# Sample queries times state with one stationary operand for all heads, and small matmuls issued as runs, in a two-layer hybrid decoder step

## The chip, the cores and the metric

The kernel runs on one core of a Trainium2 chip. The metric is the device time of one execution in microseconds (us). TensorE appears in the profile as PE (its matmuls) and PEld (the loads of its stationary operand, which overlap the matmuls), VectorE as DVE, ScalarE as ACT, GpSimd as POOL, SyncE as SP.

## The reference, cut to what matters

Two layers; each is a gated feed-forward block, a mixer of four parallel head groups, and a second feed-forward block, with a normalization ahead of each. The tokens are a prompt of 512 and a sample of 8 sequences with 8 tokens each, 576 in all; the prompt starts from an empty state, each sample sequence from a state of its own. Two head groups of the mixer (GLA with four heads of 32 keys, HGRN2 with four heads of 64 keys) follow this recurrence, in chunks:

```python
def step(S, inp):
    qc, kc, vc, gc = inp
    b = jnp.cumsum(gc, axis=1)
    o = jnp.einsum('blhk,bhkv->blhv', qc * jnp.exp(b), S)
    ...
    o = o + jnp.einsum('bijh,bjhv->bihv', att, vc)
    w_end = jnp.exp(b[:, -1:] - b)
    S = S * jnp.exp(b[:, -1])[..., None] + jnp.einsum('bjhk,bjhv->bhkv', kc * w_end, vc)
    return S, o
```

The first `einsum`, queries times the old state, is for the sample one small product for each sequence and head. A third group (SSD) has a recurrence of the same kind, a fourth is a pooling.

## The kernel before, in words

Activations lie with channels on the 128 partitions and tokens along the free dimension. Every large product is made of three matmuls, because each operand is split into a high and a low part (`whi`, `wlo`, and two planes of the activations): lines 255 to 257 (`gemm`), and lines 594 to 596 for the projections that put tokens on the partitions (`proj_tokens`). These are called large matmuls below: 128 rows by 128 columns of the array, 256 to 320 columns streamed. Weights are loaded by DMA and split by ACT (line 194) and DVE (line 195).

In each mixer two generators are interleaved. One is a chain of small dependent steps (`gla`, later `ssd`), the other is a fill of large matmuls (`fill_gla`, `fill_ssd`). After each piece of the fill some steps of the chain are recorded inside `tc.high_priority(offset=...)`; a scheduler then writes one fixed instruction list for each engine, by the instructions' priorities and by when it thinks that their inputs are ready. TensorE works through its list in order.

The chain `gla` goes over five chunks in the order 0, 4, 1, 2, 3; chunk 4 holds the 64 sample tokens, the others 128 prompt tokens. For each chunk `levels` builds the causal weights by doubling block widths: `masked_level` (lines 1157, 1159; widths 1 to 16), lines 1032 and 1034 (widths 32 and 64), and after each level DVE updates `Qg`, `Qh`, `k` and `tree` (lines 1041 to 1048). The diagonal's products are lines 1009 and 1011. Then `finish` handles the chunk before: it transposes the keys (`kt`, lines 1079 and 1077), multiplies weights with values (line 1089) and queries with the old state (line 1091), and forms the state's update (`pu`, line 1111; for the sample line 1133).

Queries times old state of the sample stand at the end of `levels` for chunk 4, line 1063. The state of a head group lies as 128 rows of keys by 64 values for each sequence (`Ss[:, si, b]`; `si` 0 is GLA with all four heads stacked, 1 and 2 are HGRN2 with two heads each). `Qg` and `Qh` hold one copy of the queries for each head, zero in the rows of the other heads, so one stationary operand serves all heads of a group. Before, the heads of even and odd number are written to the lower and the upper 64 partitions of the output, and so each `Ss[:, si, b]` is loaded twice, once for each half: 2 x 3 x 8 = 48 matmuls in a layer, which stream 16 or 8 columns. Their stationary operand is 64 columns wide; others in these steps are 32, 64 or 128 columns wide. ACT copies the result to `ye` (line 1064); DVE scales the sample's state in place only after all 48 have read it (line 1135).

A matmul of float32 operands outside the large ones runs as two passes, two records in the trace; a transpose and the bfloat16 mask product are one.

Of the kernel before, what the change touches and what calls it, by code (L numbers as in the profile page):

```python
# [14 lines left out]
P = 128  # L15
D = 1024
KD = D // P
SEQ = 512
# [18 lines left out]
SSD_AHEAD = 60  # L37
EARLY = 5
# [68 lines left out]
class Trunk:  # L107
# [586 lines left out]

    def fill_gla(self, l, h, gp, vg, vh, xbc, gates):
        nc, I, O = self.nc, self.I, self.O
        v = self.vec[:, l]
        yield
        for dst in (vg, vh):
            self.proj_tokens(h, dst)  # L700
            yield
        yield
        past = gp.tile([P, 6, NB, 3], F32, name="sconv")
        nc.sync.dma_start(past, I["sconv"][l])
        new = gp.tile([P, 6, NB + 1, 3], F32, name="nconv")
        for i in range(6):
            ext = gp.tile([P, EXTC], F32, name="ext", bufs=2)
            nc.gpsimd.memset(ext[:, 0:3], 0.0)
            es = self.ext_sample(ext, 3)
            nc.gpsimd.tensor_copy(es[:, :, 0:3], past[:, i])  # L710
            for hf, t0, n, ps in self.proj(h):
                self.evict_ext(ext, 3, ps, hf, n)
            nc.gpsimd.tensor_copy(new[:, i, 0], ext[:, SEQ:SEQ + 3])
            nc.gpsimd.tensor_copy(new[:, i, 1:], es[:, :, LS:LS + 3])
            acc = gp.tile([P, EXTC - 3], F32, name="acc")
            m = EXTC - 3
            cw = v[:, V_CW + 4 * i:V_CW + 4 * i + 4]
            nc.scalar.activation(acc, ext[:, 0:m], AF.Copy, scale=cw[:, 0:1])
            for q in range(1, 4):
                nc.vector.scalar_tensor_tensor(acc, ext[:, q:q + m], cw[:, q:q + 1], acc, ALU.mult, ALU.add)  # L720
            c = xbc[i]
            b = v[:, V_CB + i:V_CB + i + 1]
            nc.scalar.activation(c[:, :SEQ], acc[:, :SEQ], AF.Silu, bias=b)
            nc.scalar.activation(c[:, SEQ:].rearrange("p (b q) -> p b q", q=LS),
                                 self.ext_rows(acc), AF.Silu, bias=b)
            yield
        nc.sync.dma_start(O["nconv"][l], new)
        for g in gates:
            for hf, t0, n, ps in self.proj(h):
                nc.scalar.activation(g[:, t0:t0 + n], ps[:, :n], AF.Silu)  # L730
            yield
# [84 lines left out]
    def ssd_sample(self, Ss, ye, Cf):  # L816

        nc = self.nc
        ys = self.bank()
        for g in range(2):  # L820
            for b in range(NB):
                k = slice(g * 64 + b * LS, g * 64 + b * LS + LS)
                nc.tensor.matmul(ys[:, k], Ss[:, b, P * g:P * g + P],
                                 Cf[g][:, SEQ + b * LS:SEQ + b * LS + LS], start=True, stop=True)
        nc.scalar.copy(ye, ys[:, :P])

    def ssd(self, l, sp, pre, xbc, Ss, ye):
# [13 lines left out]
        for c in (0, 4, 1, 2, 3):  # L841
# [4 lines left out]
            for t in range(2):  # L846
                nc.tensor.transpose(xt[:n, P * t:P * t + P], xs[t][:, q], self.ident)
                nc.tensor.transpose(xt[:n, 256 + P * t:256 + P * t + P], Bf[t][:, q], self.ident)
            wt = self.bank()
            nc.tensor.transpose(wt[:n, 0:8], W8[:, q], self.ident[64:72, 64:72])  # L850
# [15 lines left out]
            nc.tensor.matmul(pe4, L8[:, q], rx[:, :, :n], start=True, stop=False)  # L866
            nc.tensor.matmul(pe4, self.identb[:n, :n],
                             (self.smask if smp else self.cmask)[:n, :n].unsqueeze(1).to_broadcast([n, 4, n]),
                             start=False, stop=True)
# [3 lines left out]
            for g in range(2):  # L873
                nc.tensor.matmul(cb[:n, g * n:g * n + n], Bf[g][:, q], Cf[g][:, q], start=True, stop=True)
# [5 lines left out]
            for hh in range(4):  # L880
                r0 = 64 * (hh % 2)
                nc.tensor.matmul(yi[r0:r0 + 64, (hh // 2) * n:(hh // 2) * n + n], xd[:n, hh], att[:n, hh, :n],
                                 start=True, stop=True)
            yc = sp.tile([P, 2, P], F32, name="yc")
            yi2 = yi[:, 0:2 * n].rearrange("p (t i) -> p t i", i=n)
            if c > 0:
                pd = self.bank("lv")
                for t in range(2):
                    nc.tensor.matmul(pd[:, t * n:t * n + n], sel[:, P * t:P * t + P], cum[:, q],
                                     start=True, stop=True)  # L890
                ecb = sp.tile([P, 2, P], F32, name="ecb")
                nc.scalar.activation(ecb[:, :, :n], pd[:, 0:2 * n].rearrange("p (t i) -> p t i", i=n), AF.Exp)
                if not smp:
                    ye = self.bank()
                    for g in range(2):
                        nc.tensor.matmul(ye[:, g * n:g * n + n], S[:, P * g:P * g + P], Cf[g][:, q],
                                         start=True, stop=True)
# [7 lines left out]
            if not smp:  # L905
                pu = self.bank()
                for g in range(2):
                    nc.tensor.matmul(pu[:, P * g:P * g + P], bt[:, P * g:P * g + P],
                                     xw[:, 2 * g:2 * g + 2], start=True, stop=True)
# [71 lines left out]
    def gla(self, l, gp, f3, q3, k3, vg, vh, o3):  # L981
# [8 lines left out]
        def levels(c, st):  # L990
# [18 lines left out]
            nc.tensor.matmul(sd[r, 0:4], qk[:, 0, :n], hg, start=True, stop=True)  # L1009
            for t in range(2):  # L1010
                nc.tensor.matmul(sd[r, 4 + 2 * t:6 + 2 * t], qk[:, 1 + t, :n], h2, start=True, stop=True)
# [11 lines left out]
            while w < blk:  # L1023
# [6 lines left out]
                for j0 in range(0, n if w >= 32 else 0, 2 * w):  # L1030
                    j, i = slice(j0, j0 + w), slice(j0 + w, j0 + 2 * w)
                    nc.tensor.matmul(lv[j, 0:4 * w], kc[:, 0, j], Qg[:, :, i], start=True, stop=True)
                    for t in range(2):
                        nc.tensor.matmul(lv[j, (4 + 2 * t) * w:(6 + 2 * t) * w], kc[:, 1 + t, j], Qh[:, t, :, i],
                                         start=True, stop=True)
                    nc.scalar.copy(att[j, :, i], lv[j, 0:8 * w].rearrange("p (s w) -> p s w", w=w))
# [17 lines left out]
            if smp:  # L1054
                ys = self.bank()
                y4 = ys[:, :4 * n].rearrange("p (t i) -> p t i", i=n)
                for r0 in (0, 64):
                    odd = r0 // 64
                    for t0, t1, si, Q in ((0, 2, 0, Qg[:, odd::2]), (2, 3, 1, Qh[:, 0, odd:odd + 1]),
                                          (3, 4, 2, Qh[:, 1, odd:odd + 1])):  # L1060
                        for b in range(NB):
                            k = slice(b * LS, b * LS + LS)
                            nc.tensor.matmul(y4[r0:r0 + 64, t0:t1, k], Ss[:, si, b], Q[:, :, k], start=True, stop=True)  # L1063
                nc.scalar.copy(ye, ys[:, :4 * n])
                yield

        def finish(c, st):
# [15 lines left out]
            for s in range(8):  # L1083
                t, r0 = s // 2, 64 * (s % 2)
                val = vg[c][r, 64 * s:64 * s + 64] if s < 4 else vh[c][r, 64 * (s - 4):64 * (s - 4) + 64]
                Q = Qg[:, s] if s < 4 else Qh[:, t - 2, s % 2]
                si = 0 if s < 4 else t - 1
                out = po[r0:r0 + 64, t * n:t * n + n]
# [14 lines left out]
            if not smp:  # L1103
                pu = self.bank()
                for s in range(8):
                    if s < 4:
                        rr, si, d, val = slice(32 * s, 32 * s + 32), 0, 32, vg[c][:, 64 * s:64 * s + 64]
                    else:
                        si = 1 + (s - 4) // 2
                        rr, d, val = slice(64 * (s % 2), 64 * (s % 2) + 64), 64, vh[c][:, 64 * (s - 4):64 * (s - 4) + 64]  # L1110
                    nc.tensor.matmul(pu[rr, 64 * si:64 * si + 64], kw[:, si, rr], val, start=True, stop=True)
# [41 lines left out]
    def masked_level(self, lv, r, c0, lev, n, w, kc, g2, h2v, a2):  # L1153
# [3 lines left out]
        nc.tensor.matmul(lv[r, 0:4 * half], kc[:, 0], g2, start=True, stop=True)  # L1157
        for t in range(2):
            nc.tensor.matmul(lv[r, (4 + 2 * t) * half:(6 + 2 * t) * half], kc[:, 1 + t], h2v[t],
                             start=True, stop=True)  # L1160
# [40 lines left out]
    def group_norm(self, gp, src, groups, width, finish):  # L1201
# [5 lines left out]
        for hf, (_, n) in enumerate(HALVES):  # L1207
# [4 lines left out]
            for t in range(nt):  # L1212
                sq = self.tmp.tile([P, 320], F32, name="sq", tag="sq", bufs=2)
                nc.scalar.activation(sq[:, :n], src(t, hf), AF.Square)
                for c, t0 in enumerate(toks):
                    nc.tensor.matmul(s3[:, c, per * t:per * t + per], sq[:, t0:t0 + P], sel, start=True, stop=True)
# [289 lines left out]
```

## Time and profile before

| what | value |
|---|---|
| time, median of 3 runs | 2357.5 us (2356.81 to 2359.22) |
| time of the profiled execution | 2355.57 us, span 2353.8 us |
| mean granted TensorE clock, share of full | 0.980 |
| PE busy | 2313.3 us, 98% of the span |
| DVE busy / ACT busy | 1618.1 us, 69% / 1004.7 us, 43% |
| DMA | 189.93 MB, mean 81 GB/s |

The span goes from the first to the last instruction; 1.8 us of the profiled execution lie outside it. Busy time is the union of an engine's instructions, so a busy PE need not be streaming: a matmul's record lasts longer than its share of the pipeline, and what counts is the distance from one start to the next.

### The profile page before, as it was taken

The page shows a single profiled execution, that of the slowest core. Times are in us where ns is not written, and L with a number is a line of the kernel's source. Part 1 is how long each engine was busy: PE and PEld are TensorE (multiplying, and loading weights), DVE is VectorE, ACT ScalarE, POOL GpSimd, SP SyncE. Part 2 cuts the span into 40 slices and gives each one's busy share as a digit, 9 for nine tenths or more (in the row PEclk, how much of TensorE's full clock was granted, in tenths as well). Part 3 has the DMA queues.
Part 4 walks back from the last instruction along what each step waited for, and adds up shares of the span by engine and source line. Part 5 has one row for each costly group of instructions (what it writes and reads, how often), then busy time and mean ns, then how long its engine had stood idle before and what let it go on. Part 6 is the DMA issues. An engine that isn't in the chain of part 4 may idle for free.

```text
span 2353.8 us, 40838 instructions
## 1 busy us (share of the span) xinstructions
PE 2313.3 (98%) x16817; PEld 2200.9 (94%) x16817; DVE 1618.1 (69%) x3049; ACT 1004.7 (43%) x1834; POOL 44.9 (2%) x94
## 2 busy tenths in 40 slices
PE   7999999999999999999999999999999999999997
PEld 6999999987888999999999999999778899999997
DVE  8776666746657877667697675767374778767575
ACT  3453444622434544344454343546244435434352
POOL 1000000000010000000000000000000100000000
PEclk9999999998999999999999999999799999999998
DMA  4232323201212133232313323232112131332322
GB/s 152 84 94 83 102 81 108 69 28 50 69 39 92 56 108 92 80 108 72 117 46 99 108 73 99 68 110 63 37 42 75 57 113 37 97 101 75 96 75 74
DMA packets 63147, 189.93 MB, mean 81 GB/s; under 512 B 7120, under 2 KB 13552, under 8 KB 62448
## 3 DMA queue, kind: packets, MB, share of 16 engines
q1 hardware_dynamic: 62816, 187.31, 25.1%
q8 instruction: 132, 2.16, 0.4%
q14 instruction: 55, 0.45, 0.1%
q10 hardware_dynamic: 144, 0.00, 0.0%
HBM read 180.36 MB, written 6.93 MB: 80 GB/s over the span
## 4 chain that ended last, share of the span: by engine, by line
PE 89%; DVE 6%; ACT 3%; DMA 2%; issue 1%; ACTq 0%; DVEq 0%; SPq 0%
PE mm L257 20%; PE mm L255 20%; PE mm L256 20%; PE lv L255 3%; PE lv L257 3%; PE lv L256 3%; DVE wlo L195 2%; PE ms L257 2%; PE ms L256 2%; PE ms L255 2%; DMA raw<-wts 1%; ACT whi L194 1%; PE mm L595 1%; PE mm L596 1%; PE mm L594 1%; PE ms L1063 1%
## 5 line engine op out<-in xcount | busy, mean ns | idle before, releaser
L255 PE MATMUL mm<-h,whi 128*128 128x288 f32 (+2 forms) x1872 | 566.9, 304 | 11.8 <-ACT h L126 6.8
L257 PE MATMUL mm<-h,whi 128*128 128x288 f32 (+2 forms) x1872 | 562.3, 303 | 3.8 <-DVE h L127 3.8
L256 PE MATMUL mm<-h,wlo 128*128 128x288 f32 (+2 forms) x1872 | 563.8, 302 | 0.6 <-DVE wlo L195 0.6
L195 DVE TENSOR_TENSOR wlo<-raw,whi 128x1024 fp32r<-128x1024 f32 (+2 forms) x296 | 315.9, 1069 | 224.2 <-ACT whi L194 222.9
L255 PE MATMUL mm<-a,whi 128*128 128x256 f32 (+2 forms) x1408 | 414.5, 295 | 1.7 <-ACT a L277 1.7
L257 PE MATMUL mm<-a,whi 128*128 128x256 f32 (+2 forms) x1408 | 414.1, 295 | 0.5
L256 PE MATMUL mm<-a,wlo 128*128 128x256 f32 (+2 forms) x1408 | 414.4, 294 | 0.0
L255 PEld LDWEIGHTS mm<-h,whi 128*128 128x128 f32 x1872 | 358.3, 192 | 25.2 <-issue 10.6
L194 ACT CAST whi<-raw 128x1024 fp32r<-128x1024 f32 (+2 forms) x296 | 271.9, 921 | 249.8 <-PE mm L257 195.6
L257 PEld LDWEIGHTS mm<-h,whi 128*128 128x128 f32 x1872 | 356.5, 191 | 14.7 <-issue 7.9
L256 PEld LDWEIGHTS mm<-h,wlo 128*128 128x128 f32 x1872 | 358.0, 192 | 11.9 <-issue 10.6
L194 ACT CAST whi<-raws 128x1024 fp32r<-128x1024 f32 x195 | 204.6, 1049 | 179.3 <-PE mm L257 149.2
L195 DVE TENSOR_TENSOR wlo<-raws,whi 128x1024 fp32r<-128x1024 f32 x195 | 238.1, 1221 | 55.3 <-ACT whi L194 55.0
L257 PEld LDWEIGHTS mm<-a,whi 128*128 128x128 f32 x1408 | 263.7, 188 | 4.3 <-DVE a L278 4.3
L255 PEld LDWEIGHTS mm<-a,whi 128*128 128x128 f32 x1408 | 264.7, 188 | 2.4 <-ACT a L277 2.4
L256 PEld LDWEIGHTS mm<-a,wlo 128*128 128x128 f32 x1408 | 264.7, 188 | 0.0
L429 DVE SCALAR_TENSOR_TENSOR x<-mm,x 128x320 f32<-128x320 f32 (+2 forms) x256 | 116.5, 456 | 157.7 <-PE mm L257 157.0
L255 PE MATMUL mm<-more,whi 128*128 128x288 f32 x624 | 184.8, 296 | 0.5 <-ACT u L487 0.4
L256 PE MATMUL mm<-more,wlo 128*128 128x288 f32 x624 | 184.8, 296 | 0.3 <-DVE wlo L195 0.3
L257 PE MATMUL mm<-more,whi 128*128 128x288 f32 x624 | 184.9, 297 | 0.0
L255 PEld LDWEIGHTS mm<-more,whi 128*128 128x128 f32 x624 | 117.3, 188 | 1.5 <-ACT more L277 0.7
L256 PEld LDWEIGHTS mm<-more,wlo 128*128 128x128 f32 x624 | 117.5, 188 | 0.5 <-DVE wlo L195 0.5
(334 smaller groups left out, 3967.1 us busy)
## 6 DMA issues: line engine op xcount, KB each, us to landing
raw<-wts SPq DMA_DIRECT2D x156, 512.0 KB, 3.7
raw<-wts SPq DMA_DIRECT2D x106, 384.0 KB, 3.1
raws<-wts SPq DMA_DIRECT2D x78, 512.0 KB, 4.4
raw<-wts SPq DMA_DIRECT2D x32, 256.0 KB, 2.7
x<-x SPq DMA_DIRECT2D x4, 576.0 KB, 5.2
Ss<-sssm SPq DMA_DIRECT2D x2, 1024.0 KB, 6.5
nssm_s<-Ss SPq DMA_DIRECT2D x2, 1024.0 KB, 4.1
y<-x SPq DMA_DIRECT2D x4, 320.0 KB, 2.4
```

The source lines that it names most:

```text
L194: nc.scalar.copy(hi[:, :n], src[:, :n])
L195: nc.vector.tensor_tensor(lo[:, :n], src[:, :n], hi[:, :n].bitcast(F32), ALU.subtract)
L255: mm(ps[:, :n], wh, ah, start=(first and i == 0), stop=False)
L256: mm(ps[:, :n], wl, ah, start=False, stop=False)
L257: mm(ps[:, :n], wh, al, start=False, stop=(final and i == last))
L429: self.nc.vector.scalar_tensor_tensor(x, pd[:, :n], 0.5, x, ALU.mult, ALU.add)
L594: nc.tensor.matmul(ps[:, :256], ah, wh, start=(k == 0), stop=False)
L595: nc.tensor.matmul(ps[:, :256], ah, wl, start=False, stop=False)
L596: nc.tensor.matmul(ps[:, :256], al, wh, start=False, stop=(k == KD - 1))
L1063: nc.tensor.matmul(y4[r0:r0 + 64, t0:t1, k], Ss[:, si, b], Q[:, :, k], start=True, stop=True)
```

## The change

It has two parts. The sample's queries meet the state with each `Ss[:, si, b]` loaded once: all heads of a group are streamed together (32 columns for GLA, 16 for each half of HGRN2), and the lower and the upper 64 partitions of the output now hold the sequences 0 to 3 and 4 to 7, in alternation. That makes 24 matmuls in a layer; four ACT copies put the result into the former layout of `ye` where one did. The other part puts the small matmuls of a step into `with self.burst():`, which raises their priority by 300 places, so that the scheduler writes them down next to each other; in `finish` the order within a pair of heads is changed as well, first the two products with values, then the two with the old state.

```diff
+BURST = 300
...
+    def burst(self):
+
+        return self.tc.high_priority(offset=BURST)
...
             if smp:
                 ys = self.bank()
-                y4 = ys[:, :4 * n].rearrange("p (t i) -> p t i", i=n)
-                for r0 in (0, 64):
-                    odd = r0 // 64
-                    for t0, t1, si, Q in ((0, 2, 0, Qg[:, odd::2]), (2, 3, 1, Qh[:, 0, odd:odd + 1]),
-                                          (3, 4, 2, Qh[:, 1, odd:odd + 1])):
-                        for b in range(NB):
-                            k = slice(b * LS, b * LS + LS)
-                            nc.tensor.matmul(y4[r0:r0 + 64, t0:t1, k], Ss[:, si, b], Q[:, :, k], start=True, stop=True)
-                nc.scalar.copy(ye, ys[:, :4 * n])
+                y4 = ys[:, :256].rearrange("p (s b q) -> p s b q", b=4, q=LS)
+                with self.burst():
+                    for s0, s1, si, Q in ((0, 4, 0, Qg), (4, 6, 1, Qh[:, 0]), (6, 8, 2, Qh[:, 1])):
+                        for b in (0, 4, 1, 5, 2, 6, 3, 7):
+                            r0 = 64 * (b // 4)
+                            nc.tensor.matmul(y4[r0:r0 + 64, s0:s1, b % 4], Ss[:, si, b], Q[:, :, b * LS:b * LS + LS],
+                                             start=True, stop=True)
+                y2 = ys[:, :256].rearrange("p (t odd i) -> p odd t i", odd=2, i=32)
+                yo = ye.rearrange("p (t bh i) -> p bh t i", bh=2, i=32)
+                for odd in range(2):
+                    for bh in range(2):
+                        nc.scalar.copy(yo[64 * odd:64 * odd + 64, bh], y2[64 * bh:64 * bh + 64, odd])
                 yield
...
             kt = self.bank()
-            for t in range(3):
-                if smp:
-                    nc.tensor.matmul(kt[r, P * t:P * t + P], kc[:, t], self.ident, start=True, stop=True)
-                else:
-                    nc.tensor.transpose(kt[:, P * t:P * t + P], kc[:, t], self.ident)
+            with self.burst():
+                for t in range(3):
+                    if smp:
+                        nc.tensor.matmul(kt[r, P * t:P * t + P], kc[:, t], self.ident, start=True, stop=True)
+                    else:
+                        nc.tensor.transpose(kt[:, P * t:P * t + P], kc[:, t], self.ident)
...
-            for s in range(8):
-                t, r0 = s // 2, 64 * (s % 2)
...
-                nc.tensor.matmul(out, val, att[r, s, :n], start=True, stop=(c in (0, 4)))
-                if 0 < c < 4:
-                    nc.tensor.matmul(out, S3[:, si], Q, start=False, stop=True)
-                if s == 3:
+            old = 0 < c < 4
+            for t in range(4):
+                si = max(t - 1, 0)
+                for late in range(1 + old):
+                    for s in (2 * t, 2 * t + 1):
...
+                        with self.burst():
+                            if late:
+                                nc.tensor.matmul(out, S3[:, si], Q, start=False, stop=True)
+                            else:
+                                nc.tensor.matmul(out, val, att[r, s, :n], start=True, stop=not old)
+                if t == 1:
                     yield
```

The same `with self.burst():` goes around the matmuls of lines 1009 and 1011, 1032 and 1034, 1111, 1157 and 1159 in the GLA chain, around those of `ssd` and `ssd_sample` (lines 823, 847 to 850, 866 and 867, 874, 882, 889, 896, 908) and of `group_norm` (line 1216), with nothing else altered there. The matmuls that update the sample's state (lines 928 and 1133) are not wrapped.

In the whole program the PE list has 1000 small matmuls before and 952 after. Before they stand in 364 runs between large matmuls, 174 of these of a single matmul; after in 198 runs, 24 of a single one. Where the stationary operand's width (128, 64 or 32 columns) differs from that of the matmul before, the array changes its division into column tiles: 448 times before, 232 times after.

On PE, in the first layer's mixer, where chunk 4 reaches line 1063 (`S3s` is the sample's state, `Qh` HGRN2's queries, rows with `whi` or `wlo` are large matmuls of the values' projection), the list before alternates:

```order
L1011 MATMUL ms<-cst,qk 128x2 x2
L1063 MATMUL ms<-Qh,S3s 64x8
L594 MATMUL mm<-whi,h_4552 128x256
L1063 MATMUL ms<-Qh,S3s 64x8
L595 MATMUL mm<-wlo,h_4552 128x256
L1063 MATMUL ms<-Qh,S3s 64x8
L596 MATMUL mm<-whi,h_4552 128x256
```

The same place after the change (lines are 13 to 25 higher there: 1076 is the sample's product, 1098 the transposes, 1114 weights times values, 1135 the state's update, 1184 a level):

```order
L596 MATMUL mm<-wlo,h_4557 128x256
L1076 MATMUL ms<-Qg,S3s 64x4x8
L1098 MATMUL ms<-cst,k_4683 128x128
...
L1114 MATMUL ms<-att,vg_4684 64x128 x4
...
L1076 MATMUL ms<-Qg,S3s 64x4x8 x2
L1184 MATMUL lv<-Qh,k_4683 128x128
L1135 MATMUL ms<-vg_4684,kw 32x64 x4
L1076 MATMUL ms<-Qg,S3s 64x4x8
L1076 MATMUL ms<-Qh,S3s 64x2x8 x16
L597 MATMUL mm<-whi,h_4557 128x256
```

Rows that only repeat are left out there: eight GLA loads stand among three transposes, four products with values, two level matmuls and four of the state's update, twelve changes of width in all; the sixteen HGRN2 loads follow as one piece, and no large matmul stands between the first and the last of the 24.

On PE, the finishing step of prompt chunk 2 before (`S` is the prompt's state, `att` the weights, `vg` and `vh` the values); the pattern goes on in the same way:

```order
L1079 MATMUL ms<-cst,k_4683 128x128
L256 MATMUL mm<-h_4557,wlo 128x256
L1089 MATMUL ms<-att,vg_4686 64x128
L257 MATMUL mm<-h_4557,whi 128x256
L1091 MATMUL ms<-Qg,S_5156 64x128
L1111 MATMUL ms<-vg_4686,kw 32x64 x4
L1111 MATMUL ms<-vh_4691,kw 64x64 x2
L255 MATMUL mm<-h_4522,whi 128x320
```

And after:

```order
L1098 MATMUL ms<-cst,k_4683 128x128 x2
L1114 MATMUL ms<-att,vg_4686 64x128 x2
L1112 MATMUL ms<-Qg,S_5156 64x128 x2
...
L1112 MATMUL ms<-Qh,S_5156 64x128 x2
L1098 MATMUL ms<-cst,k_4683 128x128
L258 MATMUL mm<-h_4522,whi 128x256
...
L1135 MATMUL ms<-vg_4686,kw 32x64 x4
L1135 MATMUL ms<-vh_4691,kw 64x64 x4
```

Where ten large matmuls and two level steps stood among the pieces of this step, one run holds the transposes and the sixteen products, and after seven large matmuls a second run holds the state's update.

## Rows read from the trace of the kernel before

**Rows 1.** The page: busy time by engine, and the granted clock in 40 slices.
```profile
PE 2313.3 (98%) x16817; PEld 2200.9 (94%) x16817; DVE 1618.1 (69%) x3049; ACT 1004.7 (43%) x1834; POOL 44.9 (2%) x94
...
PEclk9999999998999999999999999999799999999998
```

**Rows 2.** Busy time and granted clock by stretch of the first layer's mixer.
```profile
core 0: us, PE busy (x) PEld busy (x) DVE busy (x) ACT busy (x) POOL busy (x), PEclk, DMA share, GB/s
505.00:514.92 9.92, 9.92 (x83) 7.50 (x82) 2.81 (x9) 1.84 (x6) 0.00 (x0) 1.00 0.01 2
514.92:540.95 26.03, 26.03 (x112) 18.81 (x112) 6.24 (x7) 5.34 (x13) 0.00 (x0) 0.57 0.08 22
540.95:545.75 4.80, 4.80 (x23) 4.62 (x21) 1.49 (x5) 0.00 (x0) 0.00 (x0) 0.50 0.26 102
...
675.47:682.28 6.81, 6.81 (x27) 5.38 (x27) 5.89 (x19) 1.62 (x2) 2.33 (x2) 0.50 0.21 68
692.54:695.93 3.39, 3.39 (x15) 2.96 (x15) 1.49 (x4) 0.69 (x3) 2.06 (x2) 0.50 0.01 3
545.75:630.00 84.25, 83.71 (x586) 64.21 (x586) 62.29 (x148) 32.23 (x76) 4.34 (x18) 1.00 0.13 42
```

**Rows 3.** Line 1063 alone: its matmuls, and who waited for it.
```profile
L1063 PE MATMUL ms<-Qh,S3s x128: 202/256/276, 514.4 to 1697.4; 128*64 128x8 f32 x128
...
  DVE S3s L1135: 31.9, 2
```

**Rows 4.** Timeline of PE, large matmuls ahead of it: start, duration, instruction.
```profile
504.70 0.28 PE L595 MATMUL mm<-wlo,h 128*128 128x256 f32 x1
504.82 0.28 PE L596 MATMUL mm<-whi,h 128*128 128x256 f32 x1
```

**Rows 5.** Timeline of PE in the alternation, at full clock.
```profile
515.44 0.28 PE L1063 MATMUL ms<-Qh,S3s 128*64 128x8 f32 x2
...
515.97 0.28 PE L1063 MATMUL ms<-Qh,S3s 128*64 128x8 f32 x2
```

**Rows 6.** The same farther on; the third row is eight loads in one run.
```profile
519.51 0.38 PE L1063 MATMUL ms<-Qh,S3s 128*64 128x8 f32 x2
...
520.34 0.39 PE L1063 MATMUL ms<-Qh,S3s 128*64 128x8 f32 x2
...
536.98 1.88 PE L1063 MATMUL ms<-Qh,S3s 128*64 128x8 f32 x16
```

**Rows 7.** Timeline of PE, the finishing step of chunk 3, one run.
```profile
626.76 0.49 PE L1079 MATMUL ms<-cst,k 128*128 128x128 f32 x3
627.18 0.45 PE L1089 MATMUL ms<-att,vg 128*64 128x128 f32 x4
...
629.13 0.32 PE L1111 MATMUL ms<-vg,kw 128*32 128x64 f32 x8
629.38 0.45 PE L1111 MATMUL ms<-vh,kw 128*64 128x64 f32 x8
629.76 0.41 PE L255 MATMUL mm<-h,whi 128*128 128x320 f32 x1
```

**Rows 8.** Timeline of PE, the finishing step of chunk 2, in pieces.
```profile
606.57 0.27 PE L1079 MATMUL ms<-cst,k 128*128 128x128 f32 x1
...
612.02 0.42 PE L255 MATMUL mm<-h,whi 128*128 128x320 f32 x1
...
612.73 0.42 PE L256 MATMUL mm<-h,wlo 128*128 128x320 f32 x1
...
616.24 0.42 PE L255 MATMUL mm<-h,whi 128*128 128x320 f32 x1
```

**Rows 9.** Timeline of PE, one level step of full width.
```profile
467.64 0.61 PE L1157 MATMUL lv<-Qg,k 128*128 128x256 f32 x2
...
468.47 0.40 PE L255 MATMUL mm<-h,whi 128*128 128x320 f32 x1
```

**Rows 10.** Who PE waited for: us in total, times, longest.
```profile
PE lv L1157 <- DVE k L1046: 1.9, 5, 0.8
```

More of the change, by code (lines that the diff above doesn't have):

```diff
@@ L872, in ssd @@
             cb = self.bank()
-            for g in range(2):
-                nc.tensor.matmul(cb[:n, g * n:g * n + n], Bf[g][:, q], Cf[g][:, q], start=True, stop=True)
+            with self.burst():
+                for g in range(2):
+                    nc.tensor.matmul(cb[:n, g * n:g * n + n], Bf[g][:, q], Cf[g][:, q], start=True, stop=True)
             for g in range(2):
@@ L879, in ssd @@
             yi = self.bank("lv")
[L880 to L883, printed above, removed]
+            with self.burst():
+                for hh in range(4):
+                    r0 = 64 * (hh % 2)
+                    nc.tensor.matmul(yi[r0:r0 + 64, (hh // 2) * n:(hh // 2) * n + n], xd[:n, hh], att[:n, hh, :n],
+                                     start=True, stop=True)
             yc = sp.tile([P, 2, P], F32, name="yc")
@@ L887, in ssd @@
                 pd = self.bank("lv")
-                for t in range(2):
-                    nc.tensor.matmul(pd[:, t * n:t * n + n], sel[:, P * t:P * t + P], cum[:, q],
-                                     start=True, stop=True)
+                with self.burst():
+                    for t in range(2):
+                        nc.tensor.matmul(pd[:, t * n:t * n + n], sel[:, P * t:P * t + P], cum[:, q],
+                                         start=True, stop=True)
                 ecb = sp.tile([P, 2, P], F32, name="ecb")
@@ L894, in ssd @@
                     ye = self.bank()
[L895 to L897 removed]
+                    with self.burst():
+                        for g in range(2):
+                            nc.tensor.matmul(ye[:, g * n:g * n + n], S[:, P * g:P * g + P], Cf[g][:, q],
+                                             start=True, stop=True)
                 nc.vector.tensor_tensor(yc[:, :, :n], ecb[:, :, :n],
@@ L906, in ssd @@
                 pu = self.bank()
-                for g in range(2):
-                    nc.tensor.matmul(pu[:, P * g:P * g + P], bt[:, P * g:P * g + P],
-                                     xw[:, 2 * g:2 * g + 2], start=True, stop=True)
+                with self.burst():
+                    for g in range(2):
+                        nc.tensor.matmul(pu[:, P * g:P * g + P], bt[:, P * g:P * g + P],
+                                         xw[:, 2 * g:2 * g + 2], start=True, stop=True)
                 S4 = S.rearrange("p (h d) -> p h d", d=64)
@@ L1031, in levels @@
                     j, i = slice(j0, j0 + w), slice(j0 + w, j0 + 2 * w)
[L1032 to L1035, printed above, removed]
+                    with self.burst():
+                        nc.tensor.matmul(lv[j, 0:4 * w], kc[:, 0, j], Qg[:, :, i], start=True, stop=True)
+                        for t in range(2):
+                            nc.tensor.matmul(lv[j, (4 + 2 * t) * w:(6 + 2 * t) * w], kc[:, 1 + t, j], Qh[:, t, :, i],
+                                             start=True, stop=True)
                     nc.scalar.copy(att[j, :, i], lv[j, 0:8 * w].rearrange("p (s w) -> p s w", w=w))
@@ L1104, in finish @@
                 pu = self.bank()
[L1105 to L1111, printed above, removed]
+                with self.burst():
+                    for s in range(8):
+                        if s < 4:
+                            rr, si, d, val = slice(32 * s, 32 * s + 32), 0, 32, vg[c][:, 64 * s:64 * s + 64]
+                        else:
+                            si = 1 + (s - 4) // 2
+                            rr, d, val = slice(64 * (s % 2), 64 * (s % 2) + 64), 64, vh[c][:, 64 * (s - 4):64 * (s - 4) + 64]
+                        nc.tensor.matmul(pu[rr, 64 * si:64 * si + 64], kw[:, si, rr], val, start=True, stop=True)
                 pu3 = pu[:, 0:192].rearrange("p (t d) -> p t d", d=64)
@@ L1156, in masked_level @@
         half, nb = n // 2, n // (2 * w)
[L1157 to L1160, printed above, removed]
+        with self.burst():
+            nc.tensor.matmul(lv[r, 0:4 * half], kc[:, 0], g2, start=True, stop=True)
+            for t in range(2):
+                nc.tensor.matmul(lv[r, (4 + 2 * t) * half:(6 + 2 * t) * half], kc[:, 1 + t], h2v[t],
+                                 start=True, stop=True)
         mask = self.lmask[r, lev, c0:c0 + half].rearrange("p (o b w) -> p o b w", o=1, w=w)
@@ L1214, in group_norm @@
                 nc.scalar.activation(sq[:, :n], src(t, hf), AF.Square)
-                for c, t0 in enumerate(toks):
-                    nc.tensor.matmul(s3[:, c, per * t:per * t + per], sq[:, t0:t0 + P], sel, start=True, stop=True)
+                with self.burst():
+                    for c, t0 in enumerate(toks):
+                        nc.tensor.matmul(s3[:, c, per * t:per * t + per], sq[:, t0:t0 + P], sel, start=True, stop=True)
             r = self.tmp.tile([P, 24], F32, name="gr", tag="gr", bufs=2)
```

46 lines of the change are left out of this document (25 added, 21 removed).

## The prediction

> **What bounds the kernel now.** I read the page first: TensorE is busy for 98% of the span, DVE for 69%, ACT for 43%, so a term of the sum must be time on TensorE [rows 1]. The same page shows the granted clock at nine tenths or more almost everywhere, and at 7 in one slice that lies in the second layer's mixer. I then took the first mixer by stretches. From 514.92 to 540.95 us TensorE is busy without a gap, but only 112 matmuls start or run there and the clock is 0.57; DVE works 6.2 of the 26 us [rows 2]. TensorE is not waiting for anything; it is doing little per microsecond. The view of line 1063 names the work: the sample's queries times state. DVE waits 31.9 us for it, 16 us in each layer [rows 3].
>
> The timeline gives the price. Two large matmuls in a row start 0.12 us apart [rows 4]. In the alternation one large matmul and one 64-column load with its two passes take 515.97 - 515.44 = 0.53 us [rows 5], and 0.83 us after the clock has fallen to half [rows 6]. The load itself is not what costs: eight of them in one run, still at half clock, take 538.79 - 536.98 = 1.81 us (1.88 with the drain), so 0.11 for a pass, about 0.055 at full clock [rows 6]. What remains of the 0.53 is 0.53 - 0.12 - 2 x 0.055 = 0.30, two changes between 128 and 64 columns, 0.15 each.
>
> The finishing steps give the same comparison without the clock. Chunk 3 finds no large matmul ready beside it, and its 51 records stand in one run: 629.76 - 626.76 = 3.00 us [rows 7]. Chunk 2 does the same work in pieces, from 606.57 to 616.24, 9.67 us [rows 8]. In between stand ten large matmuls (four of 256 columns at 0.12, six of 320 at 0.15: 1.4 us) and two level steps at 468.47 - 467.64 = 0.83 [rows 9]. That leaves 9.67 - 1.4 - 1.7 = 6.6 us: the pieces cost 3.6 us.
>
> **The change, part by part.**
>
> *Sample queries.* In the stretch 514.92 to 540.95 stand 39 of the layer's 48 loads (78 of the 112 records) and some 33 large matmuls. At full clock and undisturbed those take 33 x 0.12 = 4.0 us, so the 39 loads cost 26.0 - 4.0 = 22.0. The other nine stand in the 9.92 us ahead of it [rows 2], mixed with a finishing step. Its dense price there, from the sizes above (nine large matmuls 1.1, two level steps 1.7, transposes 0.4, eight products with values at half of 629.13 - 627.18, so 1.0, the state's update 0.6 [rows 7], the diagonal 0.9) is 5.7, so 4.2 are owed to those nine and to the pieces. Behind the stretch the clock stays at half for another 4.8 us [rows 2], of which half, 2.4, is lost. Together 28.6 us a layer.
>
> After, 24 loads remain: 48 passes, without a large matmul in between, in a run with twelve changes of width. Alternating halves is cheaper than one half: the eight passes of the HGRN2 update, alternating, take 629.76 - 629.38 = 0.38 with the change at their end [rows 7], so 0.03 each. I take 48 x 0.03 = 1.4 plus 12 x 0.15 = 1.8, and 0.5 because the values' products of that step are now split over two runs: 3.7. Bounds: no overlap of the halves, 48 x 0.055 = 2.6, which is 1.2 more; and all at half clock, 48 x 0.11 = 5.3. The four ACT copies in place of one lie on an engine that works 5.3 of these 26 us and hold a result that DVE wants only steps later; nothing if that cover is there, under a microsecond a layer if not. Saved: 28.6 - 3.7 = 24.9 a layer, 49.8 in all.
>
> The Trainium skill, TensorE: Matmul & The Clock Gate, section Part 3: Packing small matmuls, says that a load of a stationary operand overlaps matmuls in flight only when the two use different groups of rows. All 24 loads use all 128 rows, so by that rule the halves would not overlap and the saving would be 2 x 1.2 = 2.4 us smaller; the trace has 0.03 against 0.055 for the same operand width and does not agree, and I follow the trace.
>
> *Finishing steps.* Chunk 2 falls from 6.6 to the dense 3.0 plus one more run (0.3) and one change (0.15): 3.1 saved. Chunk 1 stands in the same pieces before; after, the diagonal's products stand between its state updates, six more changes of width, 0.9, so 2.3. Chunk 3 was dense and is now two runs: 0.5 lost. In the sample's finishing step and in the first chunk's narrow levels lone runs are merged, twelve become five; at the 0.3 of two changes, 7 x 0.3 = 2.1. Per layer 7.0, in all 14.0.
>
> *Other wrapped steps.* Most are 128 columns wide like the large matmuls, so that merging them takes no change of width away. In the SSD steps the number of changes of width is the same within two (54 and 56 by the list). I take 0, with 4 us either way.
>
> *What comes back.* Two things are not in the sum. The clock can still fall: behind other stretches of small matmuls it stands at 0.50 for 3.4 and 6.8 us [rows 2], a loss of half of that. I take one such fall more in a mixer, 2.5 us, 5 in all (0 if none). And TensorE now reaches the next level sooner; DVE's update of `k` is what it waits for there today, 1.9 us in all [rows 10]. I take 1 us more.
>
> Sum: 49.8 + 14.0 + 0 - 5 - 1 = 57.8. The profiled execution took 2355.6, 1.8 of it outside the span and untouched; 2355.6 - 57.8 = 2297.8. It lies 1.9 below the median of the runs shown, so for a median I say **2299**.
>
> **The rivals.**
>
> *DVE sets the pace* (0.20). Levels follow one another: TensorE, then DVE's updates, then TensorE. Against it: from 545.75 to 630 DVE is busy 62.3 of 84.25 us, 74%, and with the savings there it would be some 80%; in the 26 us of the alternation it has 20 us to spare [rows 2]. For it: the 25 us a layer that go are just the ones in which DVE could catch up, and its longest wait today is 0.8 us at one level [rows 10]. There are 31 levels in a layer; 0.4 us more on each of 62 is 25 us back: 2299 + 25 = 2324.
>
> *The clock falls as long as before* (0.12). The fall began in the alternation, between 515.97 and 519.51 [rows 5, 6], and lasted to 545.75 [rows 2], some 27 us; at 0.83 for 0.53 it took about 10 of them. If the new run brings the same, 20 less the 5 counted above come back: 2298 + 15 + 1.9 = 2314. The Trainium skill, TensorE: Matmul & The Clock Gate, section Why this matters for your kernels, says that thin matmuls make the clock swing unless they are issued contiguously along the contraction, which speaks for this. In the rows here two short falls stand for it, and against it that the finishing step of chunk 3, dense as it is, lies in a stretch with the clock at 1.00 [rows 2, 7].
>
> *More than the sum* (0.08): no fall of the clock in the mixers at all, and the SSD merges worth their 4 us: 70 us, 2287.
>
> *Slower* (0.04). TensorE works in order, and a run that is written down up to 300 places earlier stands ahead of large matmuls that are ready. If DVE is late for it, those queue behind it, and the evictions that free their PSUM banks with them. To eat 58 us the 198 runs must wait 0.3 us each beyond today; at 0.35 the time is 2355.6 - 58 + 69 = 2367. Today's longest wait of that kind is 0.8 us, at five places in all [rows 10], so I give it little.
>
> *No change* (0.02): only if these waits and the saving cancel, since the new list does have half the changes of width (448 to 232).
>
> **How the numbers follow.** The forecast, 50 to 66 us off, 2291 to 2307, has 0.54. A range from 2284 to 2330 takes in the bounds of the sum, the clock rival and the DVE rival up to 0.5 us on each level; outside stay the slower cases, the worst of the DVE rival and the best of "more", about 0.13. About 0.2%, 5 us, is what a measurement of this kernel can tell from no change. Faster by more than that: 0.54 + 0.20 + 0.12 + 0.08 = 0.94; same 0.02; slower 0.04.
>
> **What the new profile would show.** Line 1076 with 48 records a layer within some 5 us, and DVE's wait for it (16 us at line 1135) gone; the clock at 0.9 or more in the slices of both mixers where 0.7 and 0.8 stand; finishing steps of chunks 1 and 2 as runs of 2 to 3.5 us; feed-forward stretches of the same length as before. Wrong would be: large matmuls that wait for DVE or ACT in the mixers for over 10 us in all, half clock for over 10 us in a mixer beyond the two falls of today, or DVE busy near 95% between the sample's product and the end of the GLA chain.

## The result, and the profile after

The changed kernel takes 2301.9 us (median of 4 runs, 2297.56 to 2308.58), the kernel before 2358.2 on the same chip (4 runs, 2356.81 to 2359.22): a ratio of 0.9764, with a 95% interval of 0.974 to 0.9789, 56 us less. The forecast was 2299 in a range from 2284 to 2330. The profiled execution is one of 2301.8 us, with a span of 2300.0.

From the page of the kernel after, the rows that answer to [rows 1]:

```profile
PE 2253.3 (98%) x16721; PEld 2168.6 (94%) x16721; DVE 1619.4 (70%) x3049; ACT 1010.7 (44%) x1844; POOL 45.6 (2%) x94
...
PEclk9999999999989999999999999999999899999998
```

TensorE is busy for 60 us less and still for 98% of a shorter span; DVE's work is the same. The slices at 7 and 8 where the sample's product stood read 9; of the three that now read 8, the first two lie in the SSD steps.

The sample's product in the kernel after, busy time and granted clock by stretch (columns as in [rows 2]), and line 1076 with its last waiter:

```profile
493.15:498.41 5.26, 5.26 (x75) 4.08 (x74) 3.42 (x13) 0.59 (x2) 0.00 (x0) 1.00 0.01 3
498.41:597.00 98.59, 97.47 (x756) 81.28 (x756) 71.03 (x165) 40.60 (x99) 5.19 (x18) 1.00 0.16 52
...
L1076 PE MATMUL ms<-Qh,S3s x64: 209/209/230, 497.0 to 1630.3; 128*64 128x16 f32 x64
...
  DVE S3s L1159: 0.5, 2
```

All 24 loads of the first layer, part of a finishing step and two level products fit into 5.3 us at a clock of 1.00, and it stays at 1.00 for the 98 us behind; before, 30.8 us went by at 0.57 and 0.50 [rows 2]. The 31.9 us for which DVE waited [rows 3] are 0.5. DVE is busy for 71.0 of those 98.6 us, 72%.

Timeline of PE after: the end of that run, then the finishing step of chunk 2, against [rows 7, 8]:

```profile
497.13 1.14 PE L1076 MATMUL ms<-Qh,S3s 128*64 128x16 f32 x31
498.19 0.38 PE L597 MATMUL mm<-whi,h 128*128 128x256 f32 x1
...
569.79 0.38 PE L1098 MATMUL ms<-cst,k 128*128 128x128 f32 x2
570.10 0.44 PE L1114 MATMUL ms<-att,vg 128*64 128x128 f32 x4
...
572.00 0.33 PE L1098 MATMUL ms<-cst,k 128*128 128x128 f32 x1
572.09 0.36 PE L258 MATMUL mm<-h,whi 128*128 128x256 f32 x1
...
573.10 0.32 PE L1135 MATMUL ms<-vg,kw 128*32 128x64 f32 x8
573.35 0.45 PE L1135 MATMUL ms<-vh,kw 128*64 128x64 f32 x8
573.73 0.39 PE L256 MATMUL mm<-h,whi 128*128 128x256 f32 x1
```

31 passes of the sample's product take 498.19 - 497.13 = 1.06 us, 0.03 each. Chunk 2's step takes 572.09 - 569.79 = 2.30 and 573.73 - 573.10 = 0.63 us, 2.9 where the pieces cost 6.6.

Not all is gain. Who PE waited for after (us in total, times, longest):

```profile
PE ms L1252 <- DVE wide L1249: 4.2, 6, 1.4
...
PE lv L1182 <- DVE k L1061: 3.3, 7, 0.8
PE lv L874 <- DVE yc L912: 2.9, 2, 2.2
```

The level's wait for `k` grew by 1.4 us [rows 10]. The other two lie in the group norm and in the SSD steps.

The stretches at half clock (a granted clock of 0.50) in the two mixers, in all, before and then after:

```profile
518.45:545.76 27.31, 27.31 (x112) 20.83 (x112) 7.05 (x10) 3.33 (x6) 0.00 (x0) 0.50 0.13 39
...
sum 75.10, PE 75.10 PEld 58.42 DVE 28.96 ACT 11.28 POOL 8.80; mean PE 12.52 PEld 9.74 DVE 4.83 ACT 1.88 POOL 1.47
```

```profile
653.45:660.28 6.83, 6.83 (x32) 6.58 (x32) 3.38 (x11) 1.06 (x4) 0.00 (x0) 0.50 0.00 0
673.93:680.76 6.83, 6.83 (x24) 5.88 (x23) 2.27 (x5) 0.60 (x1) 0.00 (x0) 0.50 0.18 58
...
sum 27.31, PE 27.31 PEld 25.86 DVE 13.95 ACT 3.10 POOL 1.92; mean PE 6.83 PEld 6.47 DVE 3.49 ACT 0.77 POOL 0.48
```

Before, 27.31 us a layer (one row of two) belong to the sample's product; that is gone. The remaining stretches lie in the SSD steps: 75.10 - 2 x 27.31 = 20.5 us before, 27.3 after. The mean granted clock of the change's four executions went from 0.988 (2308.6 us) to 0.991 (2297.6 us), so a few us of half clock come and go between executions of one kernel, and a difference of that size between two profiles shows little.

### The profile page after: what moved, and what is told of

Read it like the earlier page. It is cut to its first block, busy times and chain, and to the rows that moved or that the text cites. A ratio compares the mean times of both kernels' runs of the same rounds, so it can differ in the third digit from the quotient of the medians.

```text
span 2300.0 us, 40667 instructions
## 1 busy us (share of the span) xinstructions
PE 2253.3 (98%) x16721; PEld 2168.6 (94%) x16721; DVE 1619.4 (70%) x3049; ACT 1010.7 (44%) x1844; POOL 45.6 (2%) x94
## 4 chain that ended last, share of the span: by engine, by line
PE 88%; DVE 7%; ACT 3%; DMA 1%; issue 1%; POOL 0%; ACTq 0%; DVEq 0%; SPq 0%
PE mm L258 21%; PE mm L256 21%; PE mm L257 20%; PE lv L256 3%; PE lv L258 3%; PE lv L257 3%; PE ms L258 2%; PE ms L257 2%; PE ms L256 2%; DVE wlo L196 1%; ACT whi L195 1%; PE lv L1182 1%; DMA raw<-wts 1%; DVE att L1187 1%; PE ms L1157 1%
## 5 line engine op out<-in xcount | busy, mean ns | idle before, releaser
L256 PEld LDWEIGHTS mm<-h,whi 128*128 128x128 f32 x1872 | 357.6, 191 | 24.1 <-issue 10.6
```

Source lines behind the costliest of these rows:

```text
L256: mm(ps[:, :n], wh, ah, start=(first and i == 0), stop=False)
```

## The experiments

Each ratio is against runs of the kernel before on the same chip; the last column is the ratio less 1, times 2358.

| kernel | median us | ratio, 95% interval | us against before |
|---|---|---|---|
| half_loads | 2336.3 | 0.9905 (0.9892 to 0.9919) | -22 |
| run_of_48 | 2334.0 | 0.9897 (0.9883 to 0.9910) | -24 |
| half_loads_run | 2319.2 | 0.9825 (0.9812 to 0.9838) | -41 |
| wide_48 | 2349.1 | 0.9960 (0.9947 to 0.9972) | -9 |
| one_half_at_a_time | 2317.8 | 0.9828 (0.9814 to 0.9841) | -41 |
| old_sample_in_runs | 2320.1 | 0.9842 (0.9825 to 0.9860) | -37 |
| no_finish_runs | 2320.7 | 0.9847 (0.9833 to 0.9860) | -36 |
| the change | 2301.9 | 0.9764 (0.9740 to 0.9789) | -56 |
| no_norm_runs | 2298.6 | 0.9748 (0.9733 to 0.9764) | -59 |
| no_ssd_runs | 2294.5 | 0.9733 (0.9719 to 0.9747) | -63 |
| runs_in_gla_only | 2292.0 | 0.9719 (0.9705 to 0.9732) | -66 |
| gla_wide_12 | 2292.6 | 0.9727 (0.9712 to 0.9743) | -64 |
| gla_no_level_runs | 2287.9 | 0.9707 (0.9690 to 0.9724) | -69 |

**Loads and run, each alone.** The theory was the prediction's: a lone load among large matmuls costs two changes of width, the alternation also brings the clock down, and both loads and run count. The rivals: only the order matters, or only the number of loads.

half_loads is the kernel before with the new product, not in a run:

```diff
-                for r0 in (0, 64):
...
+                for s0, s1, si, Q in ((0, 4, 0, Qg), (4, 6, 1, Qh[:, 0]), (6, 8, 2, Qh[:, 1])):
+                    for b in (0, 4, 1, 5, 2, 6, 3, 7):
```

> The kernel before with the sample's product alone changed (24 loads in a layer in place of 48, with the four copies), and no run: the loads still alternate with large matmuls. Width theory (each lone load costs two changes of width, 0.30 us, besides its two passes, and the alternation brings the clock down): half the loads save half of 48 x 0.41 = 9.8 us a layer, and about half of the 10 us that the clock fall costs, so 30 us in all, 2328 us. Order theory (only that the loads stand in one run matters): 24 x 0.11 us less a layer, 2353 us. Load theory (only their number matters): as low as the whole change, near 2306 us.

run_of_48 is the kernel before with one line ahead of the old loops, half_loads_run has both edits:

```diff
+                with self.tc.high_priority(offset=300):
```

> The kernel before with its 48 loads of the sample's product in one run of raised priority, nothing else changed. Width theory: 96 passes at 0.055 us (blocks of one half do not alternate) and two changes of width, 5.6 us a layer in place of some 28, so 45 us less, 2313 us. Order theory: the same as with 24 loads in a run, about 2308 us. Load theory: no change, 2358 us. Clock rival (a dense run of thin matmuls lets the clock fall as long as the alternation did): 2313 + 20 = 2333 us, and a fall to half clock of some 20 us behind the run.

> The kernel before with the sample's product as after, 24 loads in one run, and no other run. Width theory: 48 passes at 0.03 to 0.055 us and two changes of width, 2 to 3 us a layer in place of some 28: 50 us less, 2308 us, so that all other runs together are worth the 6 us that then remain to the kernel after (the prediction had 14 for the finishing steps). If the finishing steps are worth 14 us: 2316 us.

Measured: -22, -24 and -41. Neither alone does it, so both rivals fall. In half_loads the alternation, though with half the loads, still stands at half clock:

```profile
519.98:533.63 13.65, 13.65 (x56) 10.48 (x56) 4.28 (x8) 3.52 (x11) 0.00 (x0) 0.50 0.00 0
```

half_loads came 8 us and half_loads_run 11 us above what was expected; for the latter 2316, the case with 14 us left to the finishing steps, was nearer. run_of_48 came out at 2334, where the clock rival stood (2333). That rival expected half clock for some 20 us behind the run, and it was 10.24, so the mechanism is there and the match to 1 us is luck. Its timeline and stretches of PE, first layer:

```profile
498.67 1.10 PE L1064 MATMUL ms<-Qg,S3s 128*64 128x16 f32 x16
499.62 1.84 PE L1064 MATMUL ms<-Qh,S3s 128*64 128x8 f32 x29
...
506.38 0.58 PE L595 MATMUL mm<-wlo,h 128*128 128x256 f32 x1
...
501.42:511.66 10.24, 10.24 (x76) 10.22 (x75) 4.06 (x16) 0.74 (x2) 0.00 (x0) 0.50 0.12 46
```

Sixteen passes take 499.62 - 498.67 = 0.95 us, 0.059 each; then the clock falls to 0.50 within the run, and the run lasts 506.38 - 498.67 = 7.7 us, with half clock for 10.24. half_loads_run, first its run, then the ends of chunk 0's finishing step (line 1160 is a level there), then chunk 3's state update:

```profile
501.83 0.66 PE L1061 MATMUL ms<-Qg,S3s 128*64 128x32 f32 x16
502.32 1.09 PE L1061 MATMUL ms<-Qh,S3s 128*64 128x16 f32 x32
503.34 0.39 PE L595 MATMUL mm<-wlo,h 128*128 128x256 f32 x1
...
504.00:520.00 16.00, 16.00 (x128) 13.97 (x127) 8.84 (x29) 3.74 (x13) 0.00 (x0) 1.00 0.09 30
...
510.63 0.62 PE L1160 MATMUL lv<-Qg,k 128*128 128x256 f32 x2
...
518.75 0.39 PE L594 MATMUL mm<-whi,h 128*128 128x256 f32 x1
...
609.13 0.30 PE L1114 MATMUL ms<-vg,kw 128*32 128x64 f32 x2
609.36 0.39 PE L256 MATMUL mm<-h,wlo 128*128 128x256 f32 x1
609.67 0.30 PE L1114 MATMUL ms<-vg,kw 128*32 128x64 f32 x2
...
613.34 0.42 PE L257 MATMUL mm<-h,whi 128*128 128x320 f32 x1
```

48 passes take 503.34 - 501.83 = 1.5 us and the clock stays at 1.00 behind them. So the halved loads save the passes and the clock fall that a run of 96 still brings. The lower rows matter below. Chunk 0's step still stands in pieces here, without any load of the sample: 518.75 - 510.63 = 8.1 us with two level steps, the diagonal and eight large matmuls in it. Chunk 3's update, dense before [rows 7], alternates here, 4.2 us from 609.13 to 613.34 with seven large matmuls in it.

**The change of width by itself.** wide_48 keeps the order of before and loads two sequences at once.

```diff
-    nc.tensor.matmul(y4[r0:r0 + 64, t0:t1, k], Ss[:, si, b], Q[:, :, k], start=True, stop=True)
+    nc.tensor.matmul(y4[:, t0:t1, k], Ss[:, si, min(b, 6):min(b, 6) + 2], Q[:, :, k], start=True, stop=True)
```

> The kernel before with the order of its instruction list kept, 48 loads a layer between large matmuls, but each load takes two sequences of the state, 128 columns instead of 64, so that the array keeps its width beside the large matmuls (half of the sample's result is then of the wrong sequence; its time is what counts). Width theory: a load among large matmuls costs 0.53 - 0.12 - 0.30 = 0.11 us, 5.3 us a layer in place of some 28, and the clock stays up: 2358 - 45 = 2313 us. Rival (a small float32 load costs 0.41 us beside a large matmul whatever its width): 2358 us, with 0.53 us from load to load as before.

Measured: -9 us, far from the 45. The rows of its timeline and its half clock:

```profile
516.83 0.28 PE L1063 MATMUL ms<-Qh,S3s 128*128 128x8 f32 x2
...
517.17 0.28 PE L1063 MATMUL ms<-Qh,S3s 128*128 128x8 f32 x2
...
534.64 3.42 PE L1063 MATMUL ms<-Qh,S3s 128*128 128x8 f32 x16
537.90 0.56 PE L255 MATMUL mm<-h,whi 128*128 128x256 f32 x1
...
517.70:541.59 23.89, 23.89 (x113) 23.89 (x114) 5.58 (x6) 4.65 (x11) 0.00 (x0) 0.50 0.16 45
```

From load to load it is 0.34 us at full clock, not 0.53 and not the expected 0.23. Two mistakes were in the expectation. A pass with 128 columns costs more than one with 64: (537.90 - 534.64) / 16 = 0.20 at half clock, an estimated 0.10 at full. Two of these and a large matmul are 0.12 + 0.20 = 0.32 of the 0.34, so nothing is left for a change of width that isn't made, and an estimate of 0.30 for two changes stands. And the clock fell all the same, for 23.89 us: the alternation brings it down without changes of width.

The Trainium skill, TensorEngine Tiling (Array Packing), section Key Properties, says that changing the tiling mode drains TensorE; 0.53 us with a change against 0.34 without is in line with that.

**Halves that alternate.** one_half_at_a_time is half_loads_run with `for b in range(NB)`.

> The kernel with the sample's 24 loads in one run and nothing else changed, with the sequences in order 0 to 7, so that four loads in a row write one half of the output's partitions. If passes that alternate halves overlap: 0.055 to 0.06 us for a pass in place of 0.03, 48 passes, 1.3 us a layer, 2.6 us in all, 2322 us. If halves that alternate do not overlap (all loads use all 128 rows): the same as with alternation, 2319 us, and the same distance from pass to pass in the timeline. If the longer run also brings the clock down: 2330 us.

Measured: the same as half_loads_run. Its run in the timeline:

```profile
499.63 0.74 PE L1061 MATMUL ms<-Qg,S3s 128*64 128x32 f32 x13
...
501.50 0.39 PE L595 MATMUL mm<-wlo,h 128*128 128x256 f32 x1
```

It takes 1.87 us against 1.51, 0.039 us a pass: between strict alternation (0.03) and one half alone (0.059). So blocks of four still overlap in part, and the 0.7 us that this costs in two layers is below what these runs can tell. By the rule of the Trainium skill that the prediction weighed (TensorE: Matmul & The Clock Gate, section Part 3: Packing small matmuls), the three would be alike, since all use the same rows; the rows do not agree.

**What each group of runs is worth.** old_sample_in_runs is the change with the old 48 loads in a run. The others are the change without `with self.burst():` in some steps; no_finish_runs keeps the changed order within a pair of heads.

> The kernel after with the old 48 loads of the sample's product, in a run; all other runs stay. If a load in a run costs only its passes (96 at 0.059 against 48 at 0.03 us): 4.2 us a layer more, 2310 us. If the longer run brings the clock down behind it, as the run of 48 in the kernel before did for 10.24 us: 5 us a layer more on top, 2320 us. Order theory (only the run matters): 2302 us.

Measured 2320.1, the value for a clock fall behind the longer run. Its profile has that fall, 13.65 us in the first layer:

```profile
500.07:513.72 13.65, 13.65 (x77) 12.63 (x76) 5.53 (x15) 1.95 (x4) 0.00 (x0) 0.50 0.00 1
```

> The kernel after without runs in the finishing steps of the GLA chain; all others stay. As the prediction has it, they are worth 14 us: 2316 us. Rival (the width change costs 0.10 us, as the alternation of 128-column loads showed, and not 0.15, so each merged pair saves a third less): 2311 us. Rival (the 17 us lie in the SSD steps and the norm): 2304 us.

Measured 2320.7, above all three cases: the finishing steps' runs are worth 0.9847 - 0.9764, 20 us in place of 14 (some 13 to 26 by the two intervals).

> The kernel after without runs in the SSD steps and in the group norm; those of the GLA chain stay. As the prediction has it, the runs left out are worth 0 with 4 us either way: 2302 us, 2298 to 2306. Rival: part of the 17 us that lie between the kernel with the sample's run alone (2319) and the kernel after (2302) comes from them: 2307 to 2312 us, and the two clock falls in the SSD stretch get longer.

Measured 2292.0, faster than the change by 0.0045 of 2358, 10.6 us, and the intervals lie apart. The runs in the SSD steps and the norm are a loss. Rows of its page and its waits, and the sum of its stretches at half clock in the mixers:

```profile
PE 2250.3 (98%) x16721; PEld 2163.9 (94%) x16721; DVE 1616.4 (71%) x3049; ACT 1006.2 (44%) x1840; POOL 46.3 (2%) x94
...
PE ms L1252 <- DVE wide L1249: 1.0, 4, 0.3
...
sum 23.89, PE 23.89 PEld 18.58 DVE 18.24 ACT 6.20 POOL 6.74; mean PE 5.97 PEld 4.64 DVE 4.56 ACT 1.55 POOL 1.68
```

In span it is 2300.0 - 2291.6 = 8.4 us. The wait of line 874 is gone and that of line 1252 is 1.0, 6.1 us less; other waits grew, and TensorE's idle time as a whole falls from 2300.0 - 2253.3 = 46.7 to 2291.6 - 2250.3 = 41.3, by 5.4. The other 3.0 are busy time, of which half of 27.31 - 23.89, 1.7, would be the clock. This fits a run that is written down ahead of large matmuls, waits for DVE and holds them up. The next two kernels do not bear out that split.

> The kernel after without runs in the SSD steps; those of the GLA chain and of the group norm stay. The runs in the SSD steps and the norm together cost 10 us (2292 without them, 2302 with them). If the SSD runs are the cause (a run written down earlier stands in front of ready large matmuls and waits for DVE: 2.9 us at line 874 in the trace after, with what queues behind it): 2292 to 2295 us, and the wait of line 874 is gone. If the norm's runs are (wait of line 1252, 4.2 us after against 1.0 before): 2300 us, and the wait of line 1252 stays.

> The kernel after without runs in the group norm; those of the GLA chain and of the SSD steps stay. If the norm's runs cost the larger part of the 10 us: 2293 to 2297 us and a wait of about 1 us at line 1252 as before the change. If the SSD runs do: 2300 us, with line 1252 waiting for about 4 us and line 874 for about 3 all the same.

Without the SSD steps' runs 2294.5, without the norm's 2298.6; both intervals overlap that of the change, so the shares, some 7 and 4 us, aren't settled. Nor do the waits split as expected: that of line 874 is gone in both, that of line 1252 stays in both. First no_ssd_runs, with its half clock in the mixers, then no_norm_runs:

```profile
PE 2246.7 (98%) x16721; PEld 2162.6 (94%) x16721; DVE 1619.5 (71%) x3049; ACT 1006.4 (44%) x1840; POOL 47.4 (2%) x94
...
PE ms L1252 <- DVE wide L1249: 4.9, 6, 2.4
...
sum 17.05, PE 16.70 PEld 15.01 DVE 12.48 ACT 6.67 POOL 4.78; mean PE 3.34 PEld 3.00 DVE 2.50 ACT 1.33 POOL 0.96
```

```profile
PE 2249.6 (98%) x16721; PEld 2166.2 (94%) x16721; DVE 1623.9 (71%) x3049; ACT 1013.6 (44%) x1844; POOL 45.6 (2%) x94
...
PE ms L1252 <- DVE wide L1249: 4.4, 4, 2.0
```

In no_ssd_runs TensorE idles for 2292.0 - 2246.7 = 45.3 us, only 1.4 less than in the change, and half of 27.31 - 17.05, 5.1 us, would be the clock. In no_norm_runs it idles for 2293.6 - 2249.6 = 44.0. The wait at line 1252 can't be what makes either faster. So that these runs cost 10.6 us is measured; how much of it is waiting and how much is half clock is not settled.

> The kernel with runs in the GLA chain alone, without those of its level steps and of the diagonal; the sample's product and the finishing steps keep theirs. From the sample's run alone (2319) to this chain (2292) 27 us are unexplained by it, and the finishing steps were worth 19. If the rest is the level steps': 2300 us. As the prediction counts the merged lone runs (2.1 us a layer, partly levels): 2295 us. If a run around a level step is worth nothing: 2292 us.

Measured 2287.9, 0.0012 below runs_in_gla_only with overlapping intervals: runs around the level steps and the diagonal are worth nothing that can be told, the last case of the expectation. With runs only where the sample's product and the finishing steps are, it has the lowest time here, though several intervals overlap its own. Against half_loads_run the finishing steps' runs are worth 0.9825 - 0.9707, 28 us (some 23 to 33 by the intervals). Half of 17.06 - 10.23, 3.4 us, would be the clock (the mixers' half clock in half_loads_run and here, one profile each):

```profile
sum 17.06, PE 17.06 PEld 13.26 DVE 12.32 ACT 4.99 POOL 4.45; mean PE 5.69 PEld 4.42 DVE 4.11 ACT 1.66 POOL 1.48
```

```profile
sum 10.23, PE 10.23 PEld 8.56 DVE 6.92 ACT 2.58 POOL 3.54; mean PE 3.41 PEld 2.85 DVE 2.31 ACT 0.86 POOL 1.18
```

half_loads_run also has the old order within a pair of heads, and no kernel here takes the new order alone, so its share of the 28 is not shown.

gla_wide_12 is runs_in_gla_only with 12 loads of 128 columns, two sequences each; of each result the half that is needed is copied out:

```diff
+                        for b in range(4):
+                            nc.tensor.matmul(y4[:, s0:s1, b], Ss[:, si, 2 * b:2 * b + 2],
+                                             Q[:, :, 2 * b * LS:2 * b * LS + 2 * LS], start=True, stop=True)
```

> The kernel with runs in the GLA chain alone, and the sample's product as 12 loads a layer of 128 columns, two sequences each, of whose result one half is kept. Width theory (each change between 128 and 64 columns costs 0.10 us, and passes cost 0.06 instead of 0.03 us, but there are 24 in place of 48): up to ten changes fewer, 1 us a layer, 2 in all: 2290 us. If the change of width is free within a run: 2292 us.

Measured 2292.6, no difference from runs_in_gla_only; 2 us could not have been told.

## Why the prediction came out right, point by point

The total was right, 2301.9 for 2299, and the largest term held in mechanism and size. That the total came within 3 us is luck: the finishing steps were worth more than forecast, the other wrapped steps cost where nothing was forecast, and the two errors cancelled.

- **What bounds the kernel** held: TensorE is busy for 98% after, too.
- **Sample queries, 49.8 us.** Of this, 4.2 us a layer were owed to nine loads and to the pieces of chunk 0's finishing step together. half_loads_run parts them: without the loads that step takes 8.1 us, where the prediction's sizes give 5.6 with its eight large matmuls, so an estimated 2.5 a layer, 5 in all, are pieces. That leaves some 45 for the product. half_loads_run measured 41, with chunk 3's update newly in pieces: 4.2 less 0.9 for seven large matmuls and 0.6 dense is 2.7 a layer, 5.4 in all, so an estimated 46 for the product. The clock fall is gone as the term had it, but the changes of width are not what brings it down: in wide_48 it came without them.
- **Finishing steps, 14.0 us**, with those 5 so 19. The runs say 20 when they are taken from the change, 28 when they are added to half_loads_run. The part that was wrong is "chunk 3 loses 0.5": it took the order of before as given. Once the sample's product no longer alternates, large matmuls are ready beside chunk 3 as well, and without runs its update stands in eight pieces. The gain of one run thus depends on which others are made. Counted in the traces, the changes of width are 320 in no_finish_runs and 232 in the change, 88 fewer, but 348 in half_loads_run and 216 in gla_no_level_runs, 132 fewer; 44 more at 0.15 us are an estimated 6.6. The intervals of 20 and 28 overlap, so no more can be told.
- **Other wrapped steps, 0 with 4 either way**: the term that came out wrong. Leaving them out gains 10.6 us. That merging them takes no change of width away was right (228 in runs_in_gla_only, 232 in the change); the bound left out that a run also puts a small matmul in front of ready large ones. That mechanism was in the text, as the slower rival, with a price over all 198 runs. A loss shows for the SSD steps and the norm alone, and its split between waits and clock is open.
- **What comes back, 6 us.** The extra half clock lies in the SSD steps: half of 27.3 - 20.5, 3.4 us for 5. In the GLA chain the level's wait grew by 1.4 for 1.
- **The ratios as steps**: 41 for the product, 28 for the finishing steps, less 3 for the levels (not told from 0), less 10.6 for the other steps. They add up to the measured 56 by construction, since each kernel differs from the one before it by one group, and so do not test the terms.
- **The rivals.** DVE does not set the pace: 72% busy, and waits for `k` of 3.3 us. The clock did not fall behind the run of 24 loads, but behind a run of 48 it did, twice over (run_of_48, old_sample_in_runs), so this rival was close, and halving the loads is what kept it away. "More than the sum" is reached by gla_no_level_runs, without the SSD merges that the rival counted on. Its 70 us does not follow from its parts: no further fall and the 4 us give 57.8 + 5 + 4 = 66.8, and with the falls of today gone as well, half of 20.5 more, some 77.

## What to carry to other kernels

Small matmuls that change the width of the array are worth gathering into runs; count the changes of width in the list, and halve the passes as well, since a long run of thin passes can lose at the clock what it wins. A run of steps that are as wide as the work around them has no such price to save, and here it cost 10.6 us. Raising its priority puts it, with its waits, in front of work that is ready; that this is the cause is likely but not shown alone. Size such edits one on top of the other: the order that a profile shows is that of the kernel before, and the first edit changes what stands beside the second.

## What the runs showed of the hardware

- A pass over 64 columns takes 0.059 us in one half of the output, 0.03 when halves alternate, and 0.039 in blocks of four. One over 128 columns took 0.20 at half clock.
- From load to load in the alternation it is 0.53 us with a 64-column load between 128-column matmuls and 0.34 with a 128-column load, though its passes are dearer.
- TensorE was busy without a gap in all these stretches at a clock of 0.50: a lone load beside each large matmul (27.31 us, 23.89 with equal widths, 13.65 with half the loads) and 96 thin passes in a run (10.24). Behind 48 in a run it stayed at 1.00.
